# Mixture of softmaxes: weights multiplied on GpSimd, head 0 scaled in one op, batch 0 loaded by head

## The chip, the cores and the metric

The kernel runs on one core of a Trainium2 chip. The metric is the time of one execution on the device, in microseconds (us). Before the change it is 784.82 us (median of three runs, 784.62 to 785.87). The profile's span is 1.8 to 2.1 us shorter than this time; times inside an execution are counted from the start of the span.

DVE is VectorE, ACT is ScalarE, POOL is GpSimd, SP is the engine that issues most transfers. A DMA engine is one of the 16 engines that move data for this core; the 16 are meant wherever "DMA engine" is written, and "engine" with a name is a compute engine.

## The reference

```python
batch, seq, vocab, num_heads = 32, 128, 4096, 4
logits: (batch, seq, num_heads, vocab) float32      # 268.4 MB
prior:  (batch, seq, num_heads)        float32

prior_probs = softmax(prior, over heads)
p = softmax(logits, over vocab)
out = sum over heads of prior_probs[..., None] * p  # (batch, seq, vocab) float32, 67.1 MB
```

Every logit is read once and every output written once; nothing can be kept or shared. (The reference subtracts the maximum before each exponential; the kernels leave this out for the logits, whose values are those of a normal draw, and their results are correct.)

## The kernel before

The 128 positions lie on the 128 partitions. For each batch `b` one tile of 8.39 MB (128 x 4 heads x 4096) is loaded into one of two buffers, and each head goes through: exponential with row sum on ACT, reciprocal of the sum, product with the prior's weight, then a weighted accumulation on DVE.

```python
def pieces(b):
    return 1 if b >= B - 3 else H          # heads in one DMA: all four, but one at a time in the last 3 batches

def load(b):
    lt = lpool.tile([P, H, V], FP32, name="ltile")          # 2 buffers
    n = pieces(b)
    for h in range(0, H, n):
        nc.sync.dma_start(out=lt[:, h : h + n], in_=logits[b, :, h : h + n, :])
    ltiles[b] = lt
# ... load(0), the prior, load(1), softmax of the prior -> pp (16 transposes 32x32) ...
for b in range(B):
    last = b == B - 1
    inplace = b >= B - 2
    lt = ltiles.pop(b)
    if 0 < b < B - 3:
        store(b - 1, eng=nc.scalar)        # 2.1 MB, issued on ACT's queue
    # ... acc from a pool of two, or in place ...
    for h in range(H):
        split = last and h == H - 1
        et = lt[:, h] if inplace else epool.tile([P, V], FP32, name="etile")   # 2 buffers
        dsum = spool.tile([P, 1], FP32, name="dsum")
        nc.scalar.activation(et, lt[:, h], AF.Exp, accum_out=dsum)
        coeff = spool.tile([P, 1], FP32, name="coeff")
        rden = spool.tile([P, 1], FP32, name="rden")
        nc.vector.reciprocal(rden, dsum)
        nc.vector.tensor_mul(coeff, rden, pp[:, h, b : b + 1])
        if h == 0:
            nc.vector.tensor_scalar_mul(out=acc, in0=et, scalar1=coeff)
        elif not split:
            nc.vector.scalar_tensor_tensor(
                out=acc, in0=et, scalar=coeff, in1=acc, op0=ALU.mult, op1=ALU.add)
        # ... the very last head in 4 chunks, with a store of 1 MB after each two ...
    if b + 2 < B:
        load(b + 2)
    # ... the last stores go on SP's queue ...
```

The softmax here doesn't subtract the row's maximum and nothing guards it: scores larger than these inputs give would overflow.

## Time and profile before

| | before |
|---|---|
| time, median of 3 | 784.82 us |
| span of the profiled run | 782.8 us |
| moved by DMA | 335.68 MB |
| busy: DMA engines (queues 1 and 10) / DVE / ACT | 99.5% / 70% / 60% |
| one batch in the steady state | 24.17 us |

Parts 1 and 3 of the page of the kernel before: busy us of each engine with its share and its instructions; then for each DMA queue its packets, MB, and the time of its packets as a share of 16 engines' span.

```profile
DVE 544.9 (70%) x408; ACT 472.7 (60%) x258; POOL 0.2 (0%) x4
...
q1 hardware_dynamic: 6624, 276.83, 82.0%
q10 hardware_dynamic: 4080, 58.79, 17.5%
q14 instruction: 8, 0.07, 0.0%
```

82.0% + 17.5% leaves nothing: the kernel is bound by its DMA engines. Queue 1 carries what SP issues (46 transfers, 276.83 MB), queue 10 what ACT issues (29 transfers, 58.79 MB).

The timeline of the kernel before in the steady state (start us, duration us, engine, line, operation, out<-in, in brackets the idle time before it and what ended it):

```profile
410.17 0.17 DVE L103 RECIPROCAL rden<-dsum 128x1 f32<-128x1 f32 x1 [5.21 <-ACT etile L100]
410.37 0.16 DVE L104 TENSOR_TENSOR coeff<-rden,pp 128x1 f32<-128x1 f32 x1
412.46 2.35 DVE L106 TENSOR_SCALAR acc<-etile,coeff 128x4096 f32<-128x4096 f32 x1 [1.93 <-DMA out_dram<-acc]
414.73 0.16 DVE L103 RECIPROCAL rden<-dsum 128x1 f32<-128x1 f32 x1
414.92 0.16 DVE L104 TENSOR_TENSOR coeff<-rden,pp 128x1 f32<-128x1 f32 x1
415.11 4.49 DVE L108 SCALAR_TENSOR_TENSOR acc<-etile,coeff,acc 128x4096 f32<-128x4096 f32 x1
```

DVE waits 5.21 us for the batch's first exponential and 1.93 us for a store: it has time to spare in each batch.

### The profile page before, as it was taken

What the parts mean: (1) busy time and instruction counts of PE and PEld (TensorE: products, weight loads), DVE (VectorE), ACT (ScalarE), POOL (GpSimd) and SP (SyncE); (2) the same over time, 40 slices, a digit from 0 to 9 for tenths busy, and PEclk for the clock granted to TensorE, in tenths of its full rate; (3) what the DMA queues carried; (4) which work ended last, traced back from release to release, by engine and by line L of the source; (5) the groups of instructions that cost most, each with busy time, mean ns of one, the idle gap of its engine ahead of it and who ended that gap; (6) DMA issues with size and microseconds to landing.
All of it is one profiled execution on the core that took longest, in us unless ns stands there. A gap on an engine that the chain in (4) does not pass through costs nothing.

```text
span 782.8 us, 977 instructions
## 1 busy us (share of the span) xinstructions
DVE 544.9 (70%) x408; ACT 472.7 (60%) x258; POOL 0.2 (0%) x4
## 2 busy tenths in 40 slices
DVE  3576687666786667866678666687666876669994
ACT  0766556755567555575555765556755567558971
POOL 0000000000000000000000000000000000000000
DMA  9999999999999999999999999999999999999997
GB/s 378 429 429 448 416 454 411 456 410 457 423 417 445 447 424 442 433 424 435 422 450 422 444 423 448 419 447 419 453 414 455 421 422 443 440 414 429 428 429 334
DMA packets 10712, 335.68 MB, mean 429 GB/s; under 512 B 1200, under 2 KB 1200, under 8 KB 1232
## 3 DMA queue, kind: packets, MB, share of 16 engines
q1 hardware_dynamic: 6624, 276.83, 82.0%
q10 hardware_dynamic: 4080, 58.79, 17.5%
q14 instruction: 8, 0.07, 0.0%
HBM read 268.50 MB, written 67.11 MB: 429 GB/s over the span
## 4 chain that ended last, share of the span: by engine, by line
DMA 73%; DVE 18%; ACT 6%; issue 1%; DVEq 0%; ACTq 0%
DMA ltile<-in_logits_dram 39%; DMA out_dram<-acc 34%; DVE acc L108 10%; ACT etile L100 6%; DVE ltile L108 3%; DVE acc L106 3%; DVE ltile L106 1%; DVE coeff L104 1%; DVE ltile L114 0%; DVE rden L103 0%; DVEq L152 0%; ACTq L100 0%; ACTq L51 0%; DVEq L106 0%
## 5 line engine op out<-in xcount | busy, mean ns | idle before, releaser
L100 ACT ACTIVATE etile<-ltile 128x4096 f32<-128x4096 f32 x120 | 433.4, 3612 | 276.3 <-DMA ltile<-in_logits_dram 203.9
L108 DVE SCALAR_TENSOR_TENSOR acc<-etile,coeff,acc 128x4096 f32<-128x4096 f32 x90 | 403.6, 4484 | 3.2
L103 DVE RECIPROCAL rden<-dsum 128x1 f32<-128x1 f32 x128 | 20.2, 158 | 156.3 <-ACT etile L100 156.3
L106 DVE TENSOR_SCALAR acc<-etile,coeff 128x4096 f32<-128x4096 f32 x30 | 70.6, 2353 | 50.1 <-DMA out_dram<-acc 50.0
L100 ACT ACTIVATE ltile<-ltile 128x4096 f32<-128x4096 f32 x8 | 28.9, 3610 | 4.8 <-DMA ltile<-in_logits_dram 2.2
L104 DVE TENSOR_TENSOR coeff<-rden,pp 128x1 f32<-128x1 f32 x128 | 20.4, 159 | 4.4
L108 DVE SCALAR_TENSOR_TENSOR ltile<-ltile,coeff 128x4096 f32<-128x4096 f32 x5 | 22.4, 4485 | 0.2
L100 ACT ACTIVATION_READ_ACCUMULATOR etile<-ltile 128x1 f32 x120 | 22.4, 186 | 0.0
L60 DVE TENSOR_REDUCE pmax<-pr 32x128 f32<-32x512 f32 x1 | 0.7, 673 | 11.5 <-DMA pr<-in_prior_dram 11.5
L64 ACT ACTIVATE pe<-pc 32x512 f32<-32x512 f32 x1 | 0.6, 628 | 10.4 <-DVE pc L62 10.4
L114 DVE SCALAR_TENSOR_TENSOR ltile<-ltile,coeff 128x1024 f32<-128x1024 f32 x4 | 4.9, 1281 | 0.0
L106 DVE TENSOR_SCALAR ltile<-ltile,coeff 128x4096 f32<-128x4096 f32 x2 | 4.7, 2353 | 0.1
L64 ACT ACT_TABLE_LOAD x1 | 1.3, 1283 | 1.2 <-PEq L141 1.2
L78 DVE STREAM_TRANSPOSE pp<-pn 32x32 f32<-32x32 f32 x16 | 1.9, 170 | 0.1
L100 ACT ACTIVATION_READ_ACCUMULATOR ltile<-ltile 128x1 f32 x8 | 1.5, 186 | 0.0
L66 DVE TENSOR_REDUCE psum<-pe 32x128 f32<-32x512 f32 x1 | 0.7, 674 | 0.7 <-ACT pe L64 0.7
L71 DVE TENSOR_TENSOR pn<-pe,prec 32x512 f32<-32x512 f32 x1 | 1.0, 1021 | 0.0
L68 DVE RECIPROCAL prec<-psum 32x128 f32<-32x128 f32 x1 | 0.9, 942 | 0.0
L62 DVE TENSOR_TENSOR pc<-pr,pmax 32x512 f32<-32x512 f32 x1 | 0.7, 678 | 0.0
L141 POOL MEMSET const-bfloat16-1.0<- 128x1 bf16 x1 | 0.1, 101 | 0.0
L141 POOL MEMSET const-uint8-127<- 128x1 uint8 x1 | 0.1, 101 | 0.0
L141 POOL MEMSET const-float32-0.0<- 128x1 f32 x1 | 0.1, 98 | 0.2 <-issue 0.2
(1 smaller groups left out, 0.1 us busy)
## 6 DMA issues: line engine op xcount, KB each, us to landing
out_dram<-acc ACTq DMA_DIRECT2D x28, 2048.0 KB, 30.0
ltile<-in_logits_dram SPq DMA_DIRECT2D x12, 2048.0 KB, 22.9
out_dram<-acc SPq DMA_DIRECT2D x2, 2048.0 KB, 34.1
out_dram<-ltile SPq DMA_DIRECT2D x1, 2048.0 KB, 22.8
out_dram<-ltile SPq DMA_DIRECT2D x2, 1024.0 KB, 10.2
ltile<-in_logits_dram SPq DMA_DIRECT2D x29, 31.3
pr<-in_prior_dram ACTq DMA_DIRECT2D x1, 64.0 KB, 10.7
```

Of the source, the lines that this page charges most:

```text
L60: nc.vector.reduce_max(pmax, pr, axis=AX.X)
L62: nc.vector.tensor_sub(pc, pr, pmax.unsqueeze(2).to_broadcast([B, S, H]))
L64: nc.scalar.activation(pe, pc, AF.Exp)
L68: nc.vector.reciprocal(prec, psum)
L71: nc.vector.tensor_mul(pn.rearrange("b h s -> b s h"), pe, prec.unsqueeze(2).to_broadcast([B, S, H]))
L78: nc.vector.transpose(pp[32 * t : 32 * (t + 1), h, :], pn[:, h, 32 * t : 32 * (t + 1)])
L100: nc.scalar.activation(et, lt[:, h], AF.Exp, accum_out=dsum)
L103: nc.vector.reciprocal(rden, dsum)
L104: nc.vector.tensor_mul(coeff, rden, pp[:, h, b : b + 1])
L106: nc.vector.tensor_scalar_mul(out=acc, in0=et, scalar1=coeff)
L108: nc.vector.scalar_tensor_tensor(out=acc, in0=et, scalar=coeff, in1=acc, op0=ALU.mult, op1=ALU.add)
L114: nc.vector.scalar_tensor_tensor(out=acc[:, cs], in0=et[:, cs], scalar=coeff, in1=acc[:, cs], op0=ALU.mult, op1=ALU.add,)
```

## The change

The intent is to shorten DVE's chain: the product of reciprocal and prior weight goes to GpSimd, head 0 multiplies by the reciprocal and by the weight in one DVE pass, the sums and reciprocals lie in fixed columns, so that fewer buffers have to be waited for, and a wait between exponentials that the sum already covers is dropped. Batch 0 is loaded by head, so that work can start after a quarter of it. The first exponential of each batch is pinned behind the store of the batch before in ACT's order.

```diff
     def pieces(b):
-        return 1 if b >= B - 3 else H
+        return 1 if b == 0 or b >= B - 3 else H
 ...
-        for h in range(H):
-            nc.vector.transpose(
-                pp[32 * t : 32 * (t + 1), h, :], pn[:, h, 32 * t : 32 * (t + 1)]
-            )
+        nc.vector.transpose(
+            pp[32 * t : 32 * (t + 1)], pn[:, :, 32 * t : 32 * (t + 1)]
+        )
-    NCHUNK = 4
+    NCHUNK = 2
+    dsum = cpool.tile([P, B * H], FP32, name="dsum")       # likewise rden, coeff
+    ebuf = cpool.tile([P, 2, V], FP32, name="ebuf")
 ...
-            nc.scalar.activation(et, lt[:, h], AF.Exp, accum_out=dsum)
-            nc.vector.reciprocal(rden, dsum)
-            nc.vector.tensor_mul(coeff, rden, pp[:, h, b : b + 1])
-            if h == 0:
-                nc.vector.tensor_scalar_mul(out=acc, in0=et, scalar1=coeff)
+            ex = nc.scalar.activation(et, lt[:, h], AF.Exp, accum_out=dsum[:, col])
+            if h == 0:
+                tc.keep_in_program_order(ex)
+            if not inplace:
+                if len(exps) >= 2:
+                    tc.declare_no_dep(ex.ins, exps[-2], reason="covered by the sum")
+                exps.append(ex.ins)
+            nc.vector.reciprocal(rden[:, col], dsum[:, col])
+            if h == 0:
+                nc.vector.tensor_scalar(
+                    out=acc, in0=et, scalar1=rden[:, col], scalar2=pp[:, h, b : b + 1],
+                    op0=ALU.mult, op1=ALU.mult,
+                )
+                continue
+            nc.gpsimd.tensor_mul(coeff[:, col], rden[:, col], pp[:, h, b : b + 1])
 ...                                   # accumulation of heads 1 to 3 unchanged, coeff[:, col] as its scalar
```

More of the change, by code (lines that the diff above doesn't have):

```diff
@@ L29, with load @@
     lpool = ctx.enter_context(tc.tile_pool(name="lpool", bufs=2))
-    epool = ctx.enter_context(tc.tile_pool(name="epool", bufs=2))
     apool = ctx.enter_context(tc.tile_pool(name="apool", bufs=2))
-    spool = ctx.enter_context(tc.tile_pool(name="spool", bufs=8))
     cpool = ctx.enter_context(tc.tile_pool(name="cpool", bufs=1))
     def pieces(b):
-        return 1 if b >= B - 3 else H
+        return 1 if b == 0 or b >= B - 3 else H
     ltiles = {}
-    def load(b):
+    def load(b, eng=nc.sync):
         lt = lpool.tile([P, H, V], FP32, name="ltile")
@@ L44, in load @@
         for h in range(0, H, n):
-            nc.sync.dma_start(out=lt[:, h : h + n], in_=logits[b, :, h : h + n, :])
+            eng.dma_start(out=lt[:, h : h + n], in_=logits[b, :, h : h + n, :])
         ltiles[b] = lt
@@ L51, in store @@
         eng.dma_start(out=out[b, :, lo:hi], in_=accs[b][:, lo:hi])
-    load(0)
+    load(0, eng=nc.sync)
     pr = cpool.tile([B, S, H], FP32, name="pr")
     nc.scalar.dma_start(out=pr, in_=prior)
-    load(1)
+    load(1, eng=nc.sync)
     pmax = cpool.tile([B, S], FP32, name="pmax")
@@ L76 @@
     for t in range(S // 32):
-        for h in range(H):
-            nc.vector.transpose(
-                pp[32 * t : 32 * (t + 1), h, :], pn[:, h, 32 * t : 32 * (t + 1)]
-            )
-    NCHUNK = 4
-    CW = V // NCHUNK
+        nc.vector.transpose(
[3 more added lines that the diff above has]
+    dsum = cpool.tile([P, B * H], FP32, name="dsum")
+    rden = cpool.tile([P, B * H], FP32, name="rden")
+    coeff = cpool.tile([P, B * H], FP32, name="coeff")
+    ebuf = cpool.tile([P, 2, V], FP32, name="ebuf")
+    exps = []
     for b in range(B):
@@ L88 @@
         lt = ltiles.pop(b)
-        if 0 < b < B - 3:
-            store(b - 1, eng=nc.scalar)
         if not inplace:
@@ L95 @@
         acc = accs[b]
+        if 0 < b < B - 3:
+            store(b - 1, eng=nc.scalar)
         for h in range(H):
             split = last and h == H - 1
-            et = lt[:, h] if inplace else epool.tile([P, V], FP32, name="etile")
-            dsum = spool.tile([P, 1], FP32, name="dsum")
-            nc.scalar.activation(et, lt[:, h], AF.Exp, accum_out=dsum)
-            coeff = spool.tile([P, 1], FP32, name="coeff")
-            rden = spool.tile([P, 1], FP32, name="rden")
-            nc.vector.reciprocal(rden, dsum)
@@ L104 @@
-            nc.vector.tensor_mul(coeff, rden, pp[:, h, b : b + 1])
-            if h == 0:
-                nc.vector.tensor_scalar_mul(out=acc, in0=et, scalar1=coeff)
-            elif not split:
+            i = b * H + h
+            col = slice(i, i + 1)
+            et = lt[:, h] if inplace else ebuf[:, h % 2]
+            ex = nc.scalar.activation(et, lt[:, h], AF.Exp, accum_out=dsum[:, col])
+            if h == 0:
+                tc.keep_in_program_order(ex)
[3 more added lines that the diff above has]
+                exps.append(ex.ins)
@@ new lines @@
+            nc.vector.reciprocal(rden[:, col], dsum[:, col])
[6 more added lines that the diff above has]
+            nc.gpsimd.tensor_mul(coeff[:, col], rden[:, col], pp[:, h, b : b + 1])
+            n = NCHUNK if split else 1
+            w = V // n
+            for c in range(n):
+                cs = slice(c * w, (c + 1) * w)
@@ L108 @@
                 nc.vector.scalar_tensor_tensor(
-                    out=acc, in0=et, scalar=coeff, in1=acc, op0=ALU.mult, op1=ALU.add
-                )
-            else:
-                for c in range(NCHUNK):
-                    cs = slice(c * CW, (c + 1) * CW)
-                    nc.vector.scalar_tensor_tensor(
-                        out=acc[:, cs], in0=et[:, cs], scalar=coeff, in1=acc[:, cs],
-                        op0=ALU.mult, op1=ALU.add,
-                    )
-                    if c % 2:
-                        store(b, (c - 1) * CW, (c + 1) * CW)
+                    out=acc[:, cs], in0=et[:, cs], scalar=coeff[:, col], in1=acc[:, cs],
@@ L120 @@
+                    op0=ALU.mult, op1=ALU.add,
+                )
+                if split:
+                    store(b, c * w, (c + 1) * w)
         if b + 2 < B:
```

## The prediction

> **What bounds the kernel now: the DMA engines.** The page's queue table gives 82.0% + 17.5% = 99.5% of the 16 engines' span; DVE is busy 70%, ACT 60%. In the trace's transfer records 16 packets, one per engine, are in flight without a break from 1.7 us to about 777 us. The timeline repeats every 24.17 us (first exponentials of neighbouring batches: 382.24, 406.43, 430.61); a batch moves 8.39 MB in and 2.10 MB out, so 434 GB/s. [...] The chain of waits agrees: 73% DMA. In each batch ACT waits about 7.2 us for logits (203.9 us in all) and DVE about 5.2 us for the first exponential: both have slack.
>
> **What the change removes, adds, moves.**
> - DVE loses 128 coefficient products (159 ns, about 0.19 us start to start), 12 of 16 transposes (of 1.9 us together), two end chunks: per batch 0.76 of about 17.3 us (2.35 + 3 x 4.48 + 8 x 0.19).
> - Head 0 uses two scalars in one pass; I expect 2.35 us unchanged.
> - 96 products go to POOL: DVE reciprocal -> POOL -> DVE. The only POOL durations here are 0.10 us memsets; I estimate the product with two crossings at 0.5 to 1.2 us, where the old product took 0.19. If the order stays reciprocal, product, accumulate, the DVE cycle of heads 1 to 3 grows from 4.79 to about 5.1 to 5.8 us. A batch then takes 18 to 20 us of DVE, below 24.17.
> - Fixed columns and dropped waits: ACT's 61.2 us of buffer waits (1.1 us each) are real reuse waits behind the accumulates and mostly stay.
> - The pinned order lets store(b-1) go when its accumulator is done, about 1.5 us before the next batch lands (380.8 against 382.35); it only shifts a transfer within a full queue.
> - Batch 0 by head: first exponential near 8 to 12 us instead of 23.56, third load issued near 28 instead of 39.9, first store near 32 instead of 45.4. But no engine was idle there, so no byte moves earlier. Its packets become 16 KB (611 ns) instead of 64 KB (2418 ns): 8 x (4 x 611 - 2418) ns = 0.2 us slower.
>
> **Critical path.** Steady state: nothing. Start: about +0.2 us. End: DVE is nearly back to back from 701 to 771.5 us with 12 accumulating heads, and would end 4 to 11 us later if POOL's round trip is exposed. That is partly covered: the last store is issued at 771.6 us, but the slowest DMA engine has older work until about 778.9 and ends at 781.4, so about 6 us of lateness costs nothing. So 0 to +3 us, most likely near 0; perhaps -0.5 us from a changed imbalance between engines.
>
> **Predicted: 785.0 us, range 783.4 to 787.6.** Faster by over 2%: 0.5%; within 2%: 98.5%; slower by over 2%: 1%.
>
> **What would show each step.** DMA share again 99% or more, and 24.2 us per batch: right. First exponential before 13 us, third load before 32 us, yet batch 2's first exponential still near 68 us: the early start bought nothing. ACT's wait for logits stays the largest. POOL shows 96 small instructions; the DVE gap between reciprocal and accumulate shows the round trip. The last accumulate ends 0 to 11 us later, while the span grows less.
>
> **What would make it wrong.** A POOL round trip above 1.5 us (the end becomes DVE-bound, +5 us or more); POOL and DVE disturbing each other; two scalars halving head 0's rate (hidden until the end); 16 KB pieces arriving slower in batch 0 than at the end; an order of loads and stores that lets the queue run dry once.

## More of the kernel before

The end of the kernel before, by stretches of 2 us (stretch, length; busy time and number of instructions of DVE, ACT, POOL; clock; mean busy share of the DMA engines; GB/s):

```profile
776.00:778.00 2.00, 0.00 (x0) 0.00 (x0) 0.00 (x0) 1.00 0.97 410
778.00:780.00 2.00, 0.00 (x0) 0.00 (x0) 0.00 (x0) 1.00 0.27 115
780.00:782.00 2.00, 0.00 (x0) 0.00 (x0) 0.00 (x0) 1.00 0.04 16
```

The DMA engines do not end together: on average they are 97% busy up to 778 us, then a few are still at work, and at the last one only.

## The result

The changed kernel takes 783.28 us (median of 4 runs, 783.21 to 783.33) against 784.8 us (4 runs, 784.62 to 785.87). The ratio is 0.9978, 95% interval 0.996 to 0.9995. Ratios here are the mean time of one kernel's fast runs over that of the other's of the same rounds, so not quite the ratio of the medians quoted. It is far within 2%, but it is real, and it lies 0.1 us below the predicted range, with the sign opposite to the predicted centre (785.0).

Parts 1 and 3 of the page of the changed kernel:

```profile
DVE 527.9 (68%) x266; ACT 470.0 (60%) x258; POOL 18.6 (2%) x100
...
q1 hardware_dynamic: 7056, 276.83, 82.1%
q10 hardware_dynamic: 4080, 58.79, 17.6%
q14 instruction: 7, 0.06, 0.0%
```

The DMA engines are as full as before. DVE runs 142 instructions fewer. Queue 14 has one packet fewer.

The same part of the timeline of the changed kernel (DVE alone):

```profile
409.91 0.16 DVE L116 RECIPROCAL rden<-dsum 128x1 f32<-128x1 f32 x1 [5.90 <-ACT ebuf L107]
410.11 2.41 DVE L118 TENSOR_SCALAR acc<-ebuf,rden,pp 128x4096 f32<-128x4096 f32 x1
413.51 0.16 DVE L116 RECIPROCAL rden<-dsum 128x1 f32<-128x1 f32 x1 [0.99 <-ACT ebuf L107]
413.98 4.49 DVE L128 SCALAR_TENSOR_TENSOR acc<-ebuf,coeff,acc 128x4096 f32<-128x4096 f32 x1 [0.31 <-POOL coeff L123]
418.38 0.16 DVE L116 RECIPROCAL rden<-dsum 128x1 f32<-128x1 f32 x1
418.84 4.49 DVE L128 SCALAR_TENSOR_TENSOR acc<-ebuf,coeff,acc 128x4096 f32<-128x4096 f32 x1 [0.30 <-POOL coeff L123]
```

The trip to GpSimd and back costs DVE 0.30 us of waiting for each head, where the product itself cost about 0.19; one head's cycle (from one accumulation to the next) goes from 4.79 to 4.86 us (418.84 - 413.98). So the DVE chain became slightly longer for heads 1 to 3, and its idle time in a batch did not shrink (by the brackets 5.21 + 1.93 = 7.1 us before, 5.90 + 0.99 + 0.31 + 2 x 0.30 = 7.8 us after).

The start was rearranged as intended, and bought nothing, as predicted. In the changed kernel the first exponential starts at 8.87 us instead of 23.56, the third load is issued at 27.36 us instead of 39.60, the first store at 32.35 instead of 45.38; yet batch 2's first exponential starts at 67.81 us, against 68.12.

The end of the changed kernel, by the same stretches:

```profile
776.00:778.00 2.00, 0.00 (x0) 0.00 (x0) 0.00 (x0) 1.00 0.99 418
778.00:780.00 2.00, 0.00 (x0) 0.00 (x0) 0.00 (x0) 1.00 0.31 131
780.00:782.00 2.00, 0.00 (x0) 0.00 (x0) 0.00 (x0) 1.00 0.00 0
```

This is where the difference lies. The last accumulation ends at the same time in both kernels (766.66 + 4.87 = 771.53 and 766.92 + 4.62 = 771.54 us in the timelines). The DMA engines reach 778 us equally busy. Only the last stragglers differ.

### Reading the 16 DMA engines one by one

The trace keeps the time of every semaphore increment with which a transfer reports its end. Each of the 75 transfers of the kernel before has 16 increments (1200 in all), as many as there are DMA engines. The author reads each increment as the report of one DMA engine; read so, the 16 times of one transfer show how far the DMA engines are apart. For the last 1 MB store, sorted, in us:

```
before   778.27 778.27 778.28 778.29 778.30 778.41 778.49 778.53 778.63 778.66 779.05 779.62 779.73 780.09 780.62 781.80
after    778.44 778.45 778.48 778.59 778.69 778.70 778.89 778.98 779.07 779.11 779.11 779.16 779.80 779.83 780.30 780.38
```

The mean is 779.07 before and 779.12 after: the total of the work is the same. The last is 781.80 before and 780.38 after, 1.42 us earlier, and the span is 1.4 us shorter. **The change did not make the DMA engines' work smaller; it spread it more evenly.** In what follows, "lateness" is how far the last DMA engine of a transfer is behind the median of the 16: at the last store 3.23 us before, 1.35 us after. The trace does not say which DMA engine an increment came from, so which one is late from transfer to transfer is read from the steps of the sorted times.

### The profile page after: what moved, and what is told of

It reads as the page before. It is cut to its first block, busy times and chain, and to the rows that moved or that the text cites. A ratio compares the mean times of both kernels' runs of the same rounds, so it can differ in the third digit from the quotient of the medians.

```text
span 781.3 us, 851 instructions
## 1 busy us (share of the span) xinstructions
DVE 527.9 (68%) x266; ACT 470.0 (60%) x258; POOL 18.6 (2%) x100
## 3 DMA queue, kind: packets, MB, share of 16 engines
q1 hardware_dynamic: 7056, 276.83, 82.1%
q10 hardware_dynamic: 4080, 58.79, 17.6%
## 4 chain that ended last, share of the span: by engine, by line
DMA 66%; ACT 14%; DVE 10%; issue 7%; SPq 0%; POOL 0%; DVEq 0%; POOLq 0%; ACTq 0%
DMA ltile<-in_logits_dram 66%; ACT ebuf L107 14%; DVE acc L128 9%; DVE ltile L128 1%; SPq L43 0%; POOL coeff L123 0%; DVE rden L116 0%; DVEq L166 0%; DVE ltile L118 0%; POOLq L166 0%; ACTq L107 0%
## 5 line engine op out<-in xcount | busy, mean ns | idle before, releaser
L107 ACT ACTIVATE ebuf<-ltile 128x4096 f32<-128x4096 f32 x120 | 433.0, 3609 | 284.5 <-DMA ltile<-in_logits_dram 241.0
L128 DVE SCALAR_TENSOR_TENSOR acc<-ebuf,coeff,acc 128x4096 f32<-128x4096 f32 x90 | 403.6, 4484 | 27.4 <-POOL coeff L123 27.4
L118 DVE TENSOR_SCALAR acc<-ebuf,rden,pp 128x4096 f32<-128x4096 f32 x30 | 72.4, 2412 | 1.3 <-DVE rden L116 0.3
L123 POOL TENSOR_TENSOR coeff<-rden,pp 128x1 f32<-128x1 f32 x96 | 18.4, 191 | 748.1 <-DVE rden L116 748.1
L128 DVE SCALAR_TENSOR_TENSOR ltile<-ltile,coeff 128x4096 f32<-128x4096 f32 (+1 forms) x7 | 27.0, 3874 | 1.8 <-POOL coeff L123 1.8
L107 ACT ACTIVATION_READ_ACCUMULATOR ebuf<-ltile 128x1 f32 x120 | 22.4, 187 | 0.0
L118 DVE TENSOR_SCALAR ltile<-ltile,rden,pp 128x4096 f32<-128x4096 f32 x2 | 4.8, 2412 | 0.1
```

Of the source, the lines that this page charges most:

```text
L107: ex = nc.scalar.activation(et, lt[:, h], AF.Exp, accum_out=dsum[:, col])
L118: nc.vector.tensor_scalar(out=acc, in0=et, scalar1=rden[:, col], scalar2=pp[:, h, b : b + 1], op0=ALU.mult, op1=ALU.mult,)
L123: nc.gpsimd.tensor_mul(coeff[:, col], rden[:, col], pp[:, h, b : b + 1])
L128: nc.vector.scalar_tensor_tensor(out=acc[:, cs], in0=et[:, cs], scalar=coeff[:, col], in1=acc[:, cs], op0=ALU.mult, op1=ALU.add,)
```

## The experiments

The first theory (A) put the smaller lateness down to the start: batch 0 by head lets the first store and the loads meet in another way. Its rivals were B (DVE and GpSimd work, or the number of instructions) and C (the pinned order). Four kernels separate the parts.

**e1: the kernel before, batch 0 by head.**

```diff
-        return 1 if b >= B - 3 else H
+        return 1 if b == 0 or b >= B - 3 else H
```

> The kernel before with only batch 0 loaded by head. Theory A (the gain is a smaller spread of the 16 DMA engines at the end, born where the first store meets the loads; the earlier start-up does that): about 783.3 us, last engine of the last store about 1.4 us behind the median instead of 3.2. Rival B (the gain comes from DVE and GpSimd work or from fewer instructions): about 785.0 us, spread as before.

Measured: 784.91 us (784.76 to 785.25), ratio to before 1.0001 (0.9986 to 1.0016). Theory A falls. Batch 0 by head did make the DMA engines more even early on (lateness 0.65 us at 67 us, where the kernel before has 2.29 at 68 us), but by the end it was 3.85 us.

**e2: the changed kernel, batch 0 in one piece.** The edit is the reverse of e1.

> The changed kernel with batch 0 loaded in one piece again. Theory A: about 784.8 us, the last engine of the last store about 3 us behind the median. Rival B: about 783.1 us (0.2 us better than the changed kernel, by the larger packets).

Measured: 783.9 us (783.17 to 784.34), ratio 0.9987 (0.9972 to 1.0001). It is between the two and scatters by 1.2 us. Its best run, the profiled one, has lateness 1.23 us at the end and meets rival B; the median meets neither.

**e3: the kernel before with the pin.**

```diff
-            nc.scalar.activation(et, lt[:, h], AF.Exp, accum_out=dsum)
+            ex = nc.scalar.activation(et, lt[:, h], AF.Exp, accum_out=dsum)
+            if h == 0:
+                tc.keep_in_program_order(ex)
```

> The kernel before with only the first exponential of a batch pinned behind the store. Theory A: within 0.5 us of 784.8. Rival C (the earlier stores of the steady state make the gain): about 783.3 us.

Measured: 784.78 us (784.48 to 785.02), ratio 0.9998.

**e4: the changed kernel without the pin.**

```diff
-            if h == 0:
-                tc.keep_in_program_order(ex)
```

> The changed kernel without the pin. Theory A: about 783.3 us, unless the first store then waits for batch 1 (it would be issued at about 45 us instead of 32). Rival C: about 784.8 us.

Measured: 783.26 us (783.23 to 783.4), ratio 0.998. The pin is worth nothing in either direction; C falls.

### A new theory: instruction fetches

In e1's trace the lateness does not grow evenly. It jumps, and it jumps when queue 14 moves a packet (so in the kernel before: from 2.43 to 3.21 us at the packet of 770 us). The page calls the kind of queue 14 "instruction", and the author reads its packets as fetches of the engines' programs; f1 and f2 below test this. Eight fall within the span of the kernel before (104, 134, 319, 376, 562, 613, 741 and 770 us, rounded down as all such times here), seven within the changed kernel's (147, 168, 356, 471, 511, 737 and 749). Each packet has 8192 bytes and takes 0.31 us, and in the first six of the kernel before a 64 KB logits packet beside it is stretched from 2.42 us to 2.66 - 3.03.

Whose fetches they are can be read from the instructions in the trace, wait instructions included, that an engine has started by then. DVE has started 67, 184, 314 and 449 at four fetches of the kernel before (104, 319, 562, 770 us), and 59 and 194 at two of the changed kernel's (147, 511 us): about 128 apart. ACT has started 64, 193 and 320 at 134, 376 and 613 us before, and 65, 191 and 314 at 168, 471 and 749 us after. So ACT, which also lost 86 wait instructions by the change (410 instructions against 324), has three fetches in both kernels, and DVE has two instead of four.

Theory D: each fetch puts up to 0.9 us onto one DMA engine, and all fetches of one compute engine fall onto the same one. Since the DMA engines are hardly ever idle (99.5% busy), this lateness is kept to the end: in the kernel before, the last of the 16 stays 2.06 to 2.17 us behind the median from 114 to 555 us. DVE's program is the longest of the kernel before (408 instructions, four of the eight fetches), so the DMA engine that serves it ends last. The change took 142 instructions out of it and so two of its four fetches. Rival E: DVE's work or waits, or chance at the start. The test is to put instructions back that do nothing.

**f1 and f2: the changed kernel with 260 or 520 useless memsets on DVE** (10 or 20 for each batch, in batches 1 to 26).

```diff
+        if 1 <= b <= 26:
+            for _ in range(10):                # f2: 20
+                tc.keep_in_program_order(nc.vector.memset(junk, 0.0))
         if b + 2 < B:
             load(b + 2)
```

> The changed kernel with 260 useless 128x1 memsets on DVE, 10 at the end of each of batches 1 to 26. Theory D (each 8 KB instruction fetch of a compute engine's program puts about 0.9 us onto one DMA engine, all of DVE's onto the same one, and an engine that never idles keeps this lateness to the end): two more fetches, last engine of the last store about 3 us behind the median instead of 1.35, time about 784.9 us. Rival E (the time comes from DVE's work or waits in the loop, or from chance at the start-up): within 0.3 us of 783.3, or no pattern.

> The same with 520 memsets, 20 for each batch. Theory D: four more fetches than the changed kernel, last engine about 4.8 us behind the median, time about 786.7 us. Rival E: within 0.5 us of 783.3, since DVE still has several us of idle time in each batch.

Measured: f1 785.14 us (785.05 to 785.29), f2 787.87 us (787.29 to 788.17). f1 is 1.9 us slower than the changed kernel, and as slow as the kernel before. The changed kernel itself was timed in the first job only (a job is a set of runs made together on one chip); in f1's own job, g1 (below), which has the changed kernel's program but for two passes at the end, took 783.53 us, 1.6 us less than f1. Rival E falls. The last accumulation of f1 ends at 773.71 us, 2.2 us later than in the changed kernel, but g1 shows that being 4.1 us late there costs only 0.25 us. Part 1 and the queue's line of f1's page:

```profile
DVE 541.9 (69%) x526; ACT 470.0 (60%) x258; POOL 18.5 (2%) x100
...
q14 instruction: 9, 0.07, 0.0%
```

Two more fetches, as expected. In f1 the fetches lie at 99, 168, 269, 356, 415, 474, 585, 739 and 752 us. Five of them (168, 356, 474, 739, 752) are within 4 us of fetches of the changed kernel, so the two of the changed kernel that are gone (147, 511) and the four that are new (99, 269, 415, 585) are DVE's. Around these four, the three latest DMA engines of a transfer, in us behind the median, shortly before and after:

```
fetch at   before it           after it
  99       0.21 0.22 0.34      0.23 0.30 1.10
 269       0.29 0.57 1.02      0.29 0.54 1.97
 415       0.48 0.51 1.86      0.49 0.49 2.81
 585       0.54 1.08 2.79      0.59 1.07 3.76
```

The last of the three is the one that moves each time, by 0.8 to 1.0 us, and it does not recover. It ends 3.64 us late. ACT's or others' fetches move other DMA engines: at 474 us the second goes from 0.50 to 1.14 and the last stays (2.82, 2.80).

The kernel before shows the same steps, among others: at 562 us the two latest are 1.54 and 2.07 before the fetch, 2.05 and 2.50 after it (read as 1.54 to 2.50, while 2.07 stays); at 770 us the latest goes from 2.43 to 3.21.

f2 was slower than theory D expected (786.7). Four more fetches than the changed kernel lie within its span, as expected, but the lateness had reached 6.0 us at 760 us rather than 4.8. That is 4.65 us more than the changed kernel's 1.35, and the time is 4.6 us longer. Five of DVE's six fetches (all but the first, 0.7 us, before which it need not have been the last one) moved the last DMA engine by 0.9 to 1.0 us; a further 0.6 us came between 433 and 452 us without a fetch, and why is open. The memsets did not hold the stores back: but for the store of batch 28, each store of batches 0 to 29 is issued 0.03 us after its last accumulation, in f2 as in the changed kernel. The last stores came later too (the store of batch 30 is issued at 759.45 us, against 754.33), about as much later as the late DMA engine ends its loads, so that lateness at the last store was 4.70 us.

**f3: the same 520 memsets on GpSimd**, which is idle 98% of the time.

```diff
+                tc.keep_in_program_order(nc.gpsimd.memset(junk, 0.0))
```

> The changed kernel with 520 useless memsets on GpSimd, an engine that is idle 98% of the time, and none on DVE. Theory D: four more fetches, on whichever DMA engine serves GpSimd's program, so the last engine 3 to 4.5 us behind the median and 785 to 786.5 us. Rival E: 783.3 us.

Measured: 784.13 us (784.08 to 784.25), lateness 2.66 us. Useless work on an idle engine costs 0.85 us (0.6 us against g1 of the same job), and DVE's waits for GpSimd did not grow (27.5 us of idle time before its accumulations in `acc`, against 27.4 in the changed kernel); that speaks for D against E. The size was off: there are four more fetches, but each of GpSimd's moves its DMA engine by only 0.5 to 0.6 us (0.97 to 1.49 at 357 us, 1.92 to 2.55 at 624 us). Here a 64 KB packet beside a GpSimd fetch is stretched by 0.2 - 0.3 us in two of the five cases (93 and 624 us) and in the others not at all; beside a DVE fetch it is 0.5 us (147 and 514 us), beside an ACT fetch 0.2 - 0.3 us (165 and 471 us). Why they differ is open.

**h1: the changed kernel with the product back on DVE.** This undoes the titled part of the change alone, and no other engine's program changes but GpSimd's.

```diff
-            nc.gpsimd.tensor_mul(coeff[:, col], rden[:, col], pp[:, h, b : b + 1])
+            nc.vector.tensor_mul(coeff[:, col], rden[:, col], pp[:, h, b : b + 1])
```

> The changed kernel with only the 96 coefficient products moved back from GpSimd to DVE. Theory D: 360 DVE instructions instead of 264, so one DVE instruction fetch more (three): last engine of the last store 2.0 to 2.6 us behind the median, about 784.2 us. Rival F (moving the product is worth nothing, the gain lies in the other parts): 783.3 us.

Measured: 784.08 us (783.96 to 784.32), lateness 2.84 us. Theory D met the time to 0.1 us; the lateness is above the 2.0 to 2.6 us that it gave. In the same job p1 (below), with two DVE fetches, took 0.74 us less. The page of h1 is instructive:

```profile
DVE 543.3 (69%) x362; ACT 470.0 (60%) x258; POOL 0.2 (0%) x4
...
q14 instruction: 7, 0.06, 0.0%
```

The number of fetches is that of the changed kernel, seven. But three of them (123, 390, 632 us) are now DVE's instead of two, and GpSimd's is gone. With the total the same, h1 is 0.80 us slower than the changed kernel: by theory D what counts is how many fall on one DMA engine.

**p1: also the reciprocal on GpSimd**, as a power of -1, the version to which theory D points: four DVE instructions for each batch.

```diff
-            nc.vector.reciprocal(rden[:, col], dsum[:, col])
+            nc.gpsimd.tensor_tensor(out=rden[:, col], in0=dsum[:, col], in1=neg1, op=ALU.pow)
```

> The changed kernel with the reciprocal on GpSimd too (as a power of -1), so that DVE has four instructions for each batch. Theory D: at most one DVE fetch, at least one more of GpSimd, ScalarE's as before; last engine about 0.8 to 1.3 us behind the median, 782.6 to 783.2 us. If the longer chain on GpSimd showed: over 783.6.

Measured: 783.34 us (783.02 to 783.46), correct, lateness 1.68 us: no better than the changed kernel (783.28), and above the 782.6 to 783.2 us that theory D gave. The premise of at most one DVE fetch was wrong. The page counts 138 DVE instructions, but not those that only wait, and of these the trace has 138 instead of 41: DVE now waits for GpSimd nearly each time. With them DVE's program is 279 long instead of 310, and it still has two fetches (180 and 568 us; beside each a 64 KB packet is stretched to 2.96 us, as beside DVE's elsewhere), while GpSimd has two instead of one. The power takes GpSimd 0.55 us when DVE is idle and up to 4.6 us beside a DVE pass, 1.27 us on average. Four DMA engines end 0.9 to 1.7 us late. So p1 did not test the version that it was meant to test, but it fits theory D: 128 computing instructions fewer on DVE, the same number of its fetches, the same time. No run here beats the changed kernel beyond the scatter.

### The terms of the prediction, measured

**a1: every batch by head.** Edit: `pieces` returns 1 for every `b`.

> The changed kernel with every batch loaded by head: 16 KB packets of 611 ns in place of 64 KB packets of 2418 ns. If the predicted 0.2 us for batch 0 is right, the other 28 batches cost 28 x 0.21 = 5.9 us: about 789.2 us. If packet size costs nothing: 783.3.

Measured: 789.59 us (789.4 to 789.69). The predicted 0.2 us for each batch that is loaded in 16 KB instead of 64 KB packets is right for the other 28: they cost 6.3 us, or 0.225 us each.

**g1 and g2: the last stores late on purpose.** Two or four useless full-size DVE passes in the last batch.

```diff
             split = last and h == H - 1
+            if split:
+                for _ in range(2):             # g2: 4
+                    tc.keep_in_program_order(nc.vector.tensor_scalar_mul(
+                        out=ebuf[:, 0], in0=ebuf[:, 1], scalar1=1.0))
```

> The changed kernel with two useless full-size DVE passes (2.35 us each) ahead of the last accumulate, so that the last stores are issued 4.7 us later. If the end is bound by the work still queued on the DMA engines, as predicted: 0 to +0.8 us on 783.3. If DVE's end is what ends the kernel: +4.7 us, about 788.

> The changed kernel with four useless full-size DVE passes ahead of the last accumulate (9.6 us later). From the 4.8 us that cost 0.25 us, the queued work covers about 4.5 us: expected +4.5 to +5.5 us on 783.3, so about 788.3. If all of it were covered: 783.3.

Measured: g1 783.53 us (783.36 to 783.85), g2 784.71 us (784.66 to 784.78). g1 fits: the last accumulation ended at 775.65 us, 4.1 us late, and it cost 0.25 us. g2 missed, because the edit did not do what was meant. The scheduler put the third pass between the two halves of the last accumulation, and the fourth behind it:

```profile
771.14 2.35 DVE L132 SCALAR_TENSOR_TENSOR ltile<-ltile,coeff 128x2048 f32<-128x2048 f32 x1
773.41 2.29 DVE L106 TENSOR_SCALAR ebuf<-ebuf 128x4096 f32<-128x4096 f32 x1
775.61 2.35 DVE L132 SCALAR_TENSOR_TENSOR ltile<-ltile,coeff 128x2048 f32<-128x2048 f32 x1
777.87 2.29 DVE L106 TENSOR_SCALAR ebuf<-ebuf 128x4096 f32<-128x4096 f32 x1
```

So the last store was issued at about 778.0 us, 6.4 us late and not 9.6, and its last DMA engine landed at 781.85 us, 3.9 us later. In the changed kernel the last store is issued at 771.5 us and lands at 780.38, 8.8 us later. The difference, 5.0 us, is what lateness at the end may cost nothing; 6.4 - 5.0 = 1.4 us, and g2 is 1.43 us slower (this is no independent check, since the 5.0 us come from g2's own landing; g1's 4.1 us, nearly free, is). The prediction had put it at about 6 us.

## Why the prediction was right or wrong

**Right: what bounds the kernel, and that nothing in DVE's chain or at the start would show.** The share of the DMA engines is 99.7% after (82.1% + 17.6%), the steady state is unchanged, the first exponential comes 14.7 us earlier and batch 2's only 0.3 us, DVE's last accumulation ends at the same time, and being 4.1 us late there would have cost 0.25 us (g1).

**Right: the price of batch 0's smaller packets,** 0.2 us (a1).

**Mis-sized, without effect: GpSimd's round trip.** Predicted 0.5 to 1.2 us in place of 0.19 (the author's estimate: the trace had no GpSimd product), and up to 11 us at the end. It was 0.30 us, and DVE ended 0.01 us later: by the cycles above, three heads lose 0.07 us each in a batch, and the dropped product of head 0 gives about 0.19 us back.

**Wrong: the step "perhaps -0.5 us from a changed imbalance between engines".** The mechanism was named, but given no cause, and its size was wrong: the last DMA engine's lateness went from 3.23 to 1.35 us, worth 1.4 us on the last landing. That is nearly the whole result, so that the sum "0 to +3 us, most likely near 0" came out as -1.5 us. The prediction counted the instructions taken off DVE as time on an engine with slack ("Steady state: nothing"), and not as a shorter program to fetch. It had the means to cost this: the trace showed the slowest DMA engine ending at 781.4 us while half of the 16 were done by 778.53 us, and showed eight instruction packets. It took the imbalance as given and did not ask where it came from.

What the runs showed in its place: a fetch of DVE's program costs one DMA engine 0.8 to 1.0 us (the four of f1, and five of f2's six), and that engine keeps most of this to the end (f1 ends 3.64 us late; in e1 0.6 us of it were lost again near 710 us). The count of DVE's fetches and the time go together:

| kernel | DVE instructions | DVE fetches | lateness at the last store, us | time, us |
|---|---|---|---|---|
| changed | 266 | 2 | 1.35 | 783.28 |
| h1: product back on DVE | 362 | 3 | 2.84 | 784.08 |
| e1: before, batch 0 by head | 408 | 4 | 3.85 | 784.91 |
| f1: changed, with 260 memsets | 526 | 4 | 3.64 | 785.14 |

All four load batch 0 by head, and the other fetches hardly differ: ACT has three in each, one (737 to 739 us) was not assigned, and GpSimd has one in the changed kernel and f1 and none in the other two. One fetch more is worth 0.8 us (changed to h1, h1 to e1). The four were timed in four jobs; the kernel before ran in each of them, with medians of 784.80 (changed), 784.68 (h1), 784.73 (e1) and 785.79 us (f1). Of the 1.5 us, the product on GpSimd is 0.8 (h1). The rest fits the other fetch, by what else left DVE's program: 32 products of head 0, 12 transposes, two chunks; this part was not tested alone.

**What batch 0 by head does do.** Kernels that load it in one piece scatter: the kernel before took 784.5 to 786.8 us over all jobs, e2 783.17 to 784.34 (e3 only 784.48 to 785.02). The kernels with batch 0 by head stayed within 0.5 us each, but for f2 (0.9). In the traces the lateness after the start is 1.4 to 2.3 us in the first case (before, e2, e3 at 67 us) and 0.2 to 0.9 us in the second. That the one causes the other is likely, but was not tested on its own.

**Open.** Why a DVE fetch costs more than one of ACT or GpSimd; how the late 1.4 us that remains could be avoided; where the 0.6 us of f2's lateness came from that no fetch explains.

## What to carry to other kernels

When the DMA engines are hardly ever idle (99.5% busy here), ask not only how much they move but whether they end together: the kernel before ended with the last of the 16, 3.23 us behind the median, and small work that fell on the same one added up (four DVE fetches in f1, 3.64 us late). Instructions on an engine with plenty of idle time were not free here: 260 memsets on DVE, 69% busy, cost 1.6 us (f1 against g1), and by theory D it is their fetches that cost it; about 128 instructions of DVE, those that only wait included, cost one DMA engine 0.8 to 1.0 us. And test a plausible cause by taking it alone before believing it: the rearranged start looked like the reason, and e1 showed in one run that it was not.

## What else the traces showed

- The fetch packets have 8192 bytes, and DVE's fetches in f1 are 146 to 170 us or six to seven batches apart; DVE has started 61, 194, 308 and 441 instructions at them, waits included, so about 128 each.
- The kernel before moves 10.49 MB in 24.17 us, 434 GB/s, with one core at work.
- GpSimd's 128x1 product took 2.22 us in g1 and g2 while a full-size scalar pass of 2.29 us ran on DVE, 3.9 to 4.0 us in p1 beside an accumulation (two full-size inputs), and 0.19 us with DVE idle.
- A small GpSimd product between two DVE instructions cost DVE 0.30 us of waiting in the changed kernel, the product itself taking 0.19 us.
